# Turning x for the last stage by VectorE and DMAs instead of TensorE

## The chip, the cores and the metric

The kernel runs on one core of a Trainium2 chip. The metric is the device time of one execution in microseconds; several executions are timed and the median counts. The profile shows one execution, engine by engine: TensorE (PE, with its weight loads as PEld), VectorE (DVE), ScalarE (ACT), GpSimd (POOL) and SyncE (SP, which here only issues DMAs).

## The reference, cut to what matters

A decoder of two layers on 512 tokens of 1024 features. Each layer mixes (attention and retention) and then runs an MLP; a last RMS norm over the features of each token ends it. The change concerns the end of the second layer's MLP.

```python
D_MODEL = 1024; SEQ = 512; DEPTH = 2; D_FF = 4 * D_MODEL

def rmsnorm(x, g):
    xf = x.astype(jnp.float32)
    y = xf * lax.rsqrt(jnp.mean(xf * xf, axis=-1, keepdims=True) + EPS)
    return (y * g.astype(jnp.float32)).astype(x.dtype)

def hybrid_layer(x, g_mix, w_in, sinks, w_a, w_b, w_out, g_mlp, w_up, w_down):
    ...
    x = x + mixed @ w_out
    h2 = rmsnorm(x, g_mlp)
    x = x + jnp.square(jax.nn.relu(h2 @ w_up)) @ w_down
    return x

def reference(x, g_mix, w_in, sinks, w_a, w_b, w_out, g_mlp, w_up, w_down, g_final):
    for l in range(DEPTH):
        x = hybrid_layer(x, g_mix[l], w_in[l], sinks[l], w_a[l], w_b[l], w_out[l],
                         g_mlp[l], w_up[l], w_down[l])
    return rmsnorm(x, g_final)
```

## The kernel before, in words

All of x is kept turned: `x[:, c, :]` holds 128 features (chunk c of 8) in the partitions and the 512 tokens along the row. Weights come in units of 128x1024, 512 KB each, 46 units for `w_in` and so on in a fixed list (`unit_order`). SP loads a unit into a `raw` tile (three buffers), ACT copies it to `hi` (L286), a rounded form, DVE subtracts to get `lo` (L287), and every product is three matmuls, hi times hi, and hi times lo both ways (L332, L333, L334). Some projections are done in pairs of chunks with fewer products (`wide_pair`, L1336 and L1337): TensorE fills three PSUM banks a, b and e in turn, ACT copies b and e aside as `bu` and `eu` (L1370, L1366), copies a into b (L1363), and DVE joins them into `z` (L1343 to L1349, L1389), which is squared (L1409) and split into the two tiles of `up` (L339, L340).

The MLP of a layer goes by quarters of the 4096 hidden features. `mlp_sequence` puts them in order: for each quarter q below 3 and i from 0 to 3 first `two_chunks` for `w_down` of q, which adds two chunks of x (L1416), and then a pair of `w_up` for the next quarter. The three quarters finish all eight chunks of x but for the last quarter's share. In the second layer `end` does the last quarter with tokens in the partitions, so that the last norm can sum along rows and the output leaves by rows.

For that `end` needs x turned back. In the kernel before TensorE does it: `turned(f, b)` transposes four 128x128 pieces (L517) of half f (features 512f to 512f+511) and token block b into a PSUM bank. For f=0 ACT copies the four blocks out to `x0` (L527). Then the first half of the last stage multiplies four units of `w_down` (numbers 24 to 27, 96 matmuls) into four banks, and DVE adds them to `x0` (L550). For f=1 `seeded` copies the transposed block back into a `mm` bank (L543), on which the second half of the stage accumulates (`units` 28 to 31, split into `homes`, the tiles named r). ACT and DVE then square, scale and store. The pools: `tmp` with tag t has 6 buffers (side, eu, bu, gains, sq and others), `ps_mm` 5 banks and `ps_aux` 3.

The order on each engine is not the order of the code: a scheduler sorts all instructions by a time model of its own, and `tc.issue_after` holds one back until another has been issued. SP works strictly in its order, and a DMA that waits holds back those behind it.

Of the kernel before, what the change touches and what calls it, by code (L numbers as in the profile page):

```python
# [11 lines left out]
F32 = mybir.dt.float32  # L12
F32R = mybir.dt.float32r
AF = mybir.ActivationFunctionType
# [113 lines left out]
def decoder(ctx, tc, xT, x_first, w_in, w_a, w_b, w_out, w_up, w_down, tables, decay, band, triangles, g_last, out):  # L128
# [276 lines left out]

    def two_chunks(name, layer, moving, evacuates):

        banks = [bank(ps_mm, "mm") for _ in range(2)]
        for u in range(2):
            hi, lo = unit(name, layer)  # L410
            for j in range(4):
                k = 4 * u + j
                for c, ps in enumerate(banks):
                    cols = slice((2 * j + c) * P, (2 * j + c + 1) * P)
                    products(ps, [((hi[:, cols], lo[:, cols]), moving[k])], k == 0, k == KD - 1)
        for ps, evacuate in zip(banks, evacuates):
            evacuate(ps)
# [84 lines left out]


    def end(layer, uT):
        homes.extend(slots.four()[0] for _ in range(4))
# [6 lines left out]

        def turned(f, b, at=slice(0, T)):

            pt = bank(ps_aux, "xT")[:, : at.stop - at.start]
            for i, c in enumerate(range(at.start // P, at.stop // P)):
                nc.tensor.transpose(pt[:, i * P : (i + 1) * P], x[:, 4 * f + c, b * P : (b + 1) * P], ident)  # L517
            return pt

# [5 lines left out]

        for b in range(NB):
            nc.scalar.activation(x0[b], turned(0, b), AF.Copy)  # L527
        banks = [bank(ps_mm, "mm") for _ in range(NB)]
# [8 lines left out]

        H = T // 2
        steps = [(b, at) for b in range(NB) for at in ((slice(0, T),) if b < NB - 1 else (slice(0, H), slice(H, T)))]

        def seeded(b, at):
            ps = bank(ps_mm, "mm")[:, : at.stop - at.start]
            nc.scalar.activation(ps, turned(1, b, at), AF.Copy)  # L543
            return ps
# [3 lines left out]
        for b, ps in enumerate(banks):  # L548
            so_far = sums[b][:, 0:1]
            nc.vector.tensor_tensor(x0[b], x0[b], ps, ALU.add)  # L550
            nc.scalar.activation(temp("sq"), x0[b], AF.Square, accum_out=so_far)
            nc.vector.tensor_scalar(so_far, so_far, 1.0 / D, EPS, ALU.mult, ALU.add)
            nc.vector.tensor_tensor(x0[b], x0[b], gains[0], ALU.mult)
# [27 lines left out]
    def layer_body(layer):  # L581
# [842 lines left out]
        def first_hooks():  # L1424
# [4 lines left out]
            return {0: lambda: (rms_mlp.prepare(), sum_input(by_form, scaled_pair(0, g_mlp), 0)), 1: at1}  # L1429

        for what, q, i in mlp_sequence():
            if what == "first":
# [7 lines left out]
            elif what == "down":  # L1440
                two_chunks("w_down", layer, up[q], [put_down(2 * i), put_down(2 * i + 1)])
                if i == 3:
                    slots.give(*up_slots[q])
            elif layer == DEPTH - 1:
                end(layer, up[q])
            else:
                new_input()
                all_of(group("w_down", layer, up[q], [put_down(c, True) for c in range(4)]))
                for c in range(4, KD):
                    chunk("w_down", layer, up[q], put_down(c, True))  # L1450
                slots.give(*up_slots[q])
# [145 lines left out]
def _laid_out(x, g_mix, w_in, sinks, w_a, w_b, w_out, g_mlp, w_up, w_down, g_final):  # L1597
    r = np.arange
    wa_rows = np.concatenate([(4 * g + c) * HEAD_DIM + r(HEAD_DIM) for c in range(4) for g in range(2)])
    rotary, decay, band, triangles = _tables()  # L1600
# [38 lines left out]
```

## Time and profile before

| | us |
|---|---|
| median of 3 runs | 1473.04 |
| lowest and highest | 1472.45, 1473.24 |
| the profiled execution's own time | 1473.8 |
| its span, first to last instruction | 1472.0 |
| busy in it: PE, DVE, ACT | 1464.8, 1166.7, 810.9 |

The span is what the trace covers; the profiled execution's own time has 1.8 us more around it. A line of the timeline has the start in us from the span's start, the length, the engine, the line of the code, the operation, the tile written and the tiles read, the shape, and how often it stands there; in brackets how long the engine stood idle before it, and who ended that wait. Neighbouring matmuls overlap in the records, so TensorE's pace is read from one start to the next. The clock that TensorE was granted is 0.999 of full speed over the run.

### The profile page before, as it was taken

To read this page: it belongs to the slowest core of one execution; us is meant where nothing else is said; L and a number is where in the kernel's file an instruction comes from. 1 tells how busy PE (TensorE), PEld (TensorE's weight loads), DVE (VectorE), ACT (ScalarE), POOL (GpSimd) and SP (SyncE) were. 2 spreads that over 40 slices of the span, in tenths; PEclk is the share of its full clock that TensorE was granted. 3 is DMA by queue.
4 is the path that set the end of the run, shared out by engine and by line. 5 is a ranking of instruction groups with operands and counts; after the bars stand their busy time and mean duration, and the time that the engine had idled before them with its cause. 6 is when DMAs were issued, how large, how long until landed. Compare 5 with 4: busy or idle time off the path is not lost.

```text
span 1472.0 us, 20220 instructions
## 1 busy us (share of the span) xinstructions
PE 1464.8 (100%) x7466; PEld 1249.6 (85%) x7466; DVE 1166.7 (79%) x1920; ACT 810.9 (55%) x1306; POOL 3.8 (0%) x14
## 2 busy tenths in 40 slices
PE   9999999999999999999999999999999999999998
PEld 7888888888988888888888888888989888888887
DVE  7998878778988787776678986786899877878763
ACT  7656356654684445444455753656547754444553
POOL 0000000000000000000000000000000000000000
PEclk9999999999999999999999999999999999999999
DMA  6422843356443332333543258333654522333241
GB/s 227 127 89 92 300 158 99 102 172 212 126 126 118 101 115 93 104 104 115 165 126 97 86 186 272 104 104 102 207 171 126 154 95 93 114 106 109 90 140 57
DMA packets 71043, 194.45 MB, mean 132 GB/s; under 512 B 8457, under 2 KB 8609, under 8 KB 70945
## 3 DMA queue, kind: packets, MB, share of 16 engines
q1 hardware_dynamic: 70656, 192.65, 40.7%
q8 instruction: 58, 0.95, 0.3%
q10 hardware_dynamic: 288, 0.52, 0.1%
q14 instruction: 41, 0.33, 0.1%
HBM read 171.63 MB, written 18.89 MB: 129 GB/s over the span
## 4 chain that ended last, share of the span: by engine, by line
PE 94%; issue 5%; DMA 1%; DVE 0%; ACT 0%; POOLq 0%; DVEq 0%; SPq 0%
PE mm L334 22%; PE mm L332 22%; PE mm L333 22%; PE mm L1336 11%; PE mm L1337 5%; PE rv L332 2%; PE rv L333 2%; PE rv L334 2%; PE score L842 1%; PE r L332 1%; PE r L334 1%; PE r L333 1%; PE pT L797 0%; PE pv L823 0%; PE pv L824 0%
## 5 line engine op out<-in xcount | busy, mean ns | idle before, releaser
L333 PE MATMUL mm<-r,hi 128*128 128x512 f32 (+1 forms) x1568 | 572.5, 367 | 0.0
L332 PE MATMUL mm<-r,hi 128*128 128x512 f32 (+1 forms) x1568 | 569.7, 367 | 0.6 <-ACT r L342 0.6
L334 PE MATMUL mm<-r,lo 128*128 128x512 f32 (+1 forms) x1568 | 563.9, 367 | 0.2
L286 ACT ACTIVATE hi<-raw 128x1024 fp32r<-128x1024 f32 (+1 forms) x334 | 334.1, 1002 | 386.4 <-PE mm L333 206.8
L287 DVE TENSOR_TENSOR lo<-raw,hi 128x512 fp32r<-128x512 f32 (+1 forms) x335 | 384.7, 1151 | 111.6 <-ACT hi L286 107.9
L334 PEld LDWEIGHTS mm<-r,lo 128*128 128x128 f32 x1568 | 293.7, 188 | 48.7 <-DVE lo L287 1.4
L332 PEld LDWEIGHTS mm<-r,hi 128*128 128x128 f32 x1568 | 293.8, 188 | 47.5 <-ACT r L342 1.4
L333 PEld LDWEIGHTS mm<-r,hi 128*128 128x128 f32 x1568 | 294.3, 188 | 45.9
L1336 PE MATMUL mm<-r,hi 128*128 128x512 f32 x728 | 252.1, 391 | 0.0
L1337 PE MATMUL mm<-r,lo 128*128 128x256 f32 x728 | 200.5, 277 | 0.0
L1336 PEld LDWEIGHTS mm<-r,hi 128*128 128x128 f32 x728 | 136.5, 188 | 28.6
L1337 PEld LDWEIGHTS mm<-r,lo 128*128 128x128 f32 x728 | 136.7, 188 | 3.1 <-DVE lo L287 0.7
L1416 DVE TENSOR_TENSOR x<-x,mm 128x512 f32<-128x512 f32 x56 | 37.8, 686 | 28.9 <-PE mm L334 28.9
L1409 ACT ACTIVATE z<-z 128x512 f32<-128x512 f32 x56 | 32.4, 623 | 48.7 <-DVE z L1389 48.7
L333 PE MATMUL rv<-lo,r 128*128 128x512 f32 x128 | 49.8, 389 | 0.0
L334 PE MATMUL rv<-hi,r 128*128 128x512 f32 x128 | 49.5, 389 | 0.0
L332 PE MATMUL rv<-hi,r 128*128 128x512 f32 x128 | 49.4, 390 | 0.0
L340 DVE TENSOR_TENSOR r<-z,r 128x512 fp32r<-128x512 f32 x64 | 42.9, 686 | 3.0 <-ACT r L339 2.6
L339 ACT ACTIVATE r<-z 128x512 fp32r<-128x512 f32 x64 | 38.4, 619 | 7.9 <-DVE z L1070 7.8
L869 ACT ACTIVATE sm<-sm,st 128x256 f32<-128x256 f32 (+1 forms) x64 | 30.1, 472 | 18.9 <-DVE st L857 18.7
L1389 DVE SCALAR_TENSOR_TENSOR z<-z,rstd 128x512 f32<-128x512 f32 x52 | 35.7, 687 | 0.6
L340 DVE TENSOR_TENSOR r<-sums,r 128x1024 fp32r<-128x1024 f32 x24 | 28.9, 1220 | 0.0
(273 smaller groups left out, 1693.0 us busy)
## 6 DMA issues: line engine op xcount, KB each, us to landing
raw<-w_in_in SPq DMA_DIRECT2D x89, 512.0 KB, 3.7
raw<-w_down_in SPq DMA_DIRECT2D x64, 512.0 KB, 3.6
raw<-w_up_in SPq DMA_DIRECT2D x32, 512.0 KB, 4.0
raw<-w_up_in SPq DMA_DIRECT2D x60, 256.0 KB, 2.9
raw<-w_a_in SPq DMA_DIRECT2D x8, 512.0 KB, 4.8
ahead<-w_b_in SPq DMA_DIRECT2D x8, 512.0 KB, 5.4
park_w_b<-ahead SPq DMA_DIRECT2D x16, 256.0 KB, 5.7
ahead<-w_up_in SPq DMA_DIRECT2D x8, 512.0 KB, 4.9
```

The costliest lines, as they stand in the source:

```text
L286: nc.scalar.activation(hi[:, at], raw[:, at], AF.Copy)
L287: last_low[:] = [nc.vector.tensor_tensor(lo[:, at], raw[:, at], f32(hi[:, at]), ALU.subtract).ins]
L332: nc.tensor.matmul(ps, ah, bh, start=start and i == 0, stop=False, **more)
L333: nc.tensor.matmul(ps, ah, bl, start=False, stop=False, **more)
L334: nc.tensor.matmul(ps, al, bh, start=False, stop=stop and i == n - 1, **more)
L339: nc.scalar.activation(hi, src, AF.Copy)
L340: nc.vector.tensor_tensor(lo, src, f32(hi), ALU.subtract)
L1336: nc.tensor.matmul(both, hi[:, c], m, start=start and k == 0, stop=False, **more)
L1337: nc.tensor.matmul(ps[:, :H], lo[:, c], m[:, 0, :], start=False, stop=k == 3 and start, **more)
L1389: nc.vector.scalar_tensor_tensor(z[:, :, at], z[:, :, at], 0.0, factor, ALU.max, ALU.mult)
L1409: nc.scalar.activation(z[:, i, :], z[:, i, :], AF.Square)
L1416: nc.vector.tensor_tensor(x[:, c, :], x[:, c, :], ps, ALU.add)
```

## The change

The 32 transposes on TensorE, ACT's copies out of PSUM for f=0 and the function `turned` go. Instead `turns(f)` makes four steps. Step n takes all four chunks of half f, picks 32 tokens of each of the four token blocks, and turns them on DVE in blocks of 32x32 into a temporary tile `turned` of 128x512 (line 516 of the new code); SP writes it to a part of the HBM tensor `blocks` (line 517), 256 KB. At the fourth step SP issues four DMAs that read `blocks` back into x itself, each into 32 partitions with 4 rows of 512 values (line 520). After that x holds the half with tokens in the partitions. The 32x32 blocks leave the features in another order, so the host permutes features in `x`, `w_out`, `g_mix`, `w_in`, `g_mlp`, `w_up` and most of `w_down` such that the output comes out in its own order.

For f=0 the four steps stand behind the units of `two_chunks` for (q, i) = (2, 2) and (2, 3); for f=1 they stand at the head of `end`. DVE's addition for f=0 (line 569) and ACT's seeding for f=1 (line 562) now read x in SBUF.

```diff
-    def two_chunks(name, layer, moving, evacuates):
+    def two_chunks(name, layer, moving, evacuates, meanwhile=None):
...
+            if meanwhile:
+                with tc.issue_after(last_low[0]):
+                    meanwhile.pop(0)()
...
+    blocks = dram.tile([2, P, 4, T], F32, name="blocks")
+
+    def turns(f):
+
+        four = x[:, 4 * f : 4 * f + 4, :]
+
+        def turn(n):
+            new = temp("turned")
+            old = four.rearrange("p c (b r j) -> p c b r j", b=NB, j=32)[:, :, :, n, :]
+            nc.vector.transpose(new.rearrange("p (b c j) -> p c b j", b=NB, j=32), old)
+            nc.sync.dma_start(blocks[f, :, n, :], new)
+            if n == 3:
+                for r in range(4):
+                    nc.sync.dma_start(four[32 * r : 32 * r + 32], blocks[f, :, r, :].rearrange("(a p) w -> p a w", a=4))
+
+        return [partial(turn, n) for n in range(4)]
...
-        def turned(f, b, at=slice(0, T)):
-
-            pt = bank(ps_aux, "xT")[:, : at.stop - at.start]
-            for i, c in enumerate(range(at.start // P, at.stop // P)):
-                nc.tensor.transpose(pt[:, i * P : (i + 1) * P], x[:, 4 * f + c, b * P : (b + 1) * P], ident)
-            return pt
+        def by_rows(ap):
+            return ap.rearrange("p (a w) -> p a w", w=P)
+
+        def by_tokens(f, b):
+            return x[:, 4 * f : 4 * f + 4, b * P : (b + 1) * P]
+
+        with tc.issue_after(last_low[0]):
+            all_of(turns(1))
...
-        for b in range(NB):
-            nc.scalar.activation(x0[b], turned(0, b), AF.Copy)
...
-            nc.scalar.activation(ps, turned(1, b, at), AF.Copy)
+            nc.scalar.activation(by_rows(ps), by_tokens(1, b)[:, at.start // P : at.stop // P, :], AF.Copy)
...
-            nc.vector.tensor_tensor(x0[b], x0[b], ps, ALU.add)
+            nc.vector.tensor_tensor(by_rows(x0[b]), by_tokens(0, b), by_rows(ps), ALU.add)
...
+                if (layer, q, i) == (DEPTH - 1, 2, 2):
+                    turning = turns(0)
+                two_chunks("w_down", layer, up[q], [put_down(2 * i), put_down(2 * i + 1)], turning)
...
+    turned = r(D).reshape(2, 4, 4, 32).transpose(0, 2, 1, 3).reshape(-1)
+    x, w_out = (m[:, :, turned] for m in (x, w_out))
+    g_mix, w_in, g_mlp, w_up = (m[:, turned] for m in (g_mix, w_in, g_mlp, w_up))
```

The scheduler's order is the same up to the last 100 us or so, but for numbers in names. Lines from L403 on have moved in the new code: L1336 and L1337 of before are L1355 and L1356 there, L1363 is L1382, L1366 is L1385, L1370 is L1389 on ACT, L1389 on DVE is L1408, L1343 is L1362.

First place: the last pair (q = 3, i = 3), TensorE and ACT. TensorE before, with the banks b = mm_12719, a = mm_12720, e = mm_12721; L517 are the transposes:

```order
L1336 MATMUL mm_12720<-r12_88,hi_12660 128x512
L1337 MATMUL mm_12720<-r12_88,lo_12661 128x256
L517 MATMUL xT_12841<-ident_132,x_75 128x128 x4
L517 MATMUL xT_12847<-ident_132,x_75 128x128 x4
L517 MATMUL xT_12853<-ident_132,x_75 128x128 x4
L1336 MATMUL mm_12721<-r8_84,hi_12660 128x512
```

The same place of the change, where e is mm_12738:

```order
L1356 MATMUL mm_12737<-r12_88,lo_12668 128x256
L1355 MATMUL mm_12737<-r12_88,hi_12667 128x512
L1356 MATMUL mm_12737<-r12_88,lo_12668 128x256
L1355 MATMUL mm_12738<-r8_84,hi_12667 128x512
L1356 MATMUL mm_12738<-r8_84,lo_12668 128x256
```

Nothing stands any more between the products of bank a and those of bank e. ACT at this place before, from the copy of a into b on:

```order
L1363 ACTIVATE mm_12719<-mm_12720 128x512
L286 ACTIVATE hi_12730<-raw3_12727 128x1024
L286 ACTIVATE hi_12754<-raw_12602 128x512
L1366 ACTIVATE eu_12722<-mm_12721 128x512
L1370 ACTIVATE bu_12723<-mm_12719 128x512
L286 ACTIVATE hi_12780<-raw_12725 128x1024
```

and now:

```order
L1382 ACTIVATE mm_12736<-mm_12737 128x512
L1385 ACTIVATE eu_12739<-mm_12738 128x512
L286 ACTIVATE hi_12747<-raw3_12744 128x1024
L286 ACTIVATE hi_12771<-raw_12609 128x512
L1389 ACTIVATE bu_12740<-mm_12736 128x512
L286 ACTIVATE hi_12797<-raw_12742 128x1024
```

The copy `eu` has moved ahead of the two splits of the pair's last weights (raw3 and its neighbour).

Second place: SP from the loads of the last pair (L223 to L225) to the end of the loads. Before:

```order
L223 DMA raw<-w_up_in 128x512
L228 DMA raw_12630<-w_up_in 128x512
L225 DMA raw<-w_up_in 128x1024
L196 DMA raw<-w_down_in 128x1024 x5
L508 DMA gains<-g_last_in 128x512 x2
L196 DMA raw<-w_down_in 128x1024 x3
```

and now:

```order
L517 DMA blocks<-turned 128x512 x2
L223 DMA raw<-w_up_in 128x512
L228 DMA raw_12637<-w_up_in 128x512
L225 DMA raw<-w_up_in 128x1024
L196 DMA raw<-w_down_in 128x1024
L517 DMA blocks<-turned 128x512 x2
L520 DMA x<-blocks 32x4x512 x4
L196 DMA raw<-w_down_in 128x1024 x4
L528 DMA gains<-g_last_in 128x512 x2
L517 DMA blocks<-turned 128x512 x3
L196 DMA raw<-w_down_in 128x1024 x3
L517 DMA blocks<-turned 128x512
L520 DMA x<-blocks 32x4x512 x4
```

The four writes and four reads for f=0 stand among the loads of the last pair and of unit 25; for f=1 three writes stand ahead of the last three loads (units 29 to 31), the fourth and the four reads behind them.

Third place: DVE in the last pair, from the first norm scaling of its z on. Before:

```order
L1389 SCALAR_TENSOR_TENSOR z<-z,rstd 128x2x256
L287 TENSOR_TENSOR r_76<-raw,r_76 128x1024
L287 TENSOR_TENSOR lo<-raw,hi 128x1024
L1343 TENSOR_TENSOR z<-mm,side 128x256
L287 TENSOR_TENSOR lo<-raw,hi 128x1024
L1389 SCALAR_TENSOR_TENSOR z<-z,rstd 128x2x256
```

and now:

```order
L1408 SCALAR_TENSOR_TENSOR z<-z,rstd 128x2x256
L516 STREAM_TRANSPOSE turned<-x 128x4x4x32 x3
L287 TENSOR_TENSOR r_76<-raw,r_76 128x1024
L287 TENSOR_TENSOR lo<-raw,hi 128x1024
L1362 TENSOR_TENSOR z<-mm,side 128x256
L287 TENSOR_TENSOR lo<-raw,hi 128x1024
L516 STREAM_TRANSPOSE turned<-x 128x4x4x32
L1408 SCALAR_TENSOR_TENSOR z<-z,rstd 128x2x256
```

Three turns stand ahead of the split of unit 28 (r_76), the fourth behind that of unit 27. For f=0 the four turns stand in the same manner behind two splits each in the two pairs of steps before.

More of the change, by code (lines that the diff above doesn't have):

```diff
@@ L535, in end @@
                     multiply(ps, k, b, weights, k == 0, k == KD - 1)
-        H = T // 2
         steps = [(b, at) for b in range(NB) for at in ((slice(0, T),) if b < NB - 1 else (slice(0, H), slice(H, T)))]
@@ L1429, in first_hooks @@
             return {0: lambda: (rms_mlp.prepare(), sum_input(by_form, scaled_pair(0, g_mlp), 0)), 1: at1}
+        turning = []
         for what, q, i in mlp_sequence():
@@ L1440, in layer_body @@
             elif what == "down":
-                two_chunks("w_down", layer, up[q], [put_down(2 * i), put_down(2 * i + 1)])
+                if (layer, q, i) == (DEPTH - 1, 2, 2):
+                    turning = turns(0)
+                two_chunks("w_down", layer, up[q], [put_down(2 * i), put_down(2 * i + 1)], turning)
                 if i == 3:
@@ L1598, in _laid_out @@
     r = np.arange
+    turned = r(D).reshape(2, 4, 4, 32).transpose(0, 2, 1, 3).reshape(-1)
+    x, w_out = (m[:, :, turned] for m in (x, w_out))
+    g_mix, w_in, g_mlp, w_up = (m[:, turned] for m in (g_mix, w_in, g_mlp, w_up))
+    w_down = w_down.copy()
+    w_down[:, : 3 * D] = w_down[:, : 3 * D, turned]
+    w_down[: DEPTH - 1, 3 * D :] = w_down[: DEPTH - 1, 3 * D :, turned]
     wa_rows = np.concatenate([(4 * g + c) * HEAD_DIM + r(HEAD_DIM) for c in range(4) for g in range(2)])
```

## The prediction

> **What bounds the kernel now.** I read the page's busy time first, then the chain that ended last, then the waits of TensorE.
>
> ```profile
> span 1472.0 us, 20220 instructions
> PE 1464.8 (100%) x7466; PEld 1249.6 (85%) x7466; DVE 1166.7 (79%) x1920; ACT 810.9 (55%) x1306; POOL 3.8 (0%) x14
> PE 94%; issue 5%; DMA 1%; DVE 0%; ACT 0%; POOLq 0%; DVEq 0%; SPq 0%
> PE warm L311 <- DVE ones L306: 1.0, 1, 1.0
> PE mm L332 <- ACT r L342: 0.6, 1, 0.6
> ```
>
> TensorE is busy for the whole span, the chain lies on it for 94%, and it waits twice in 1472.0 us, for 1.0 and 0.6 us. So work taken off TensorE shortens the run by its own time, unless what feeds the matmuls behind it was only just ready. Both halves of that are worked out below: first what leaves TensorE, then whether DVE, ACT or the transfers are late for a TensorE that runs ahead.
>
> **What leaves TensorE.** The transposes are one group, and the timeline of TensorE shows the largest and one of the single ones among their neighbours (start, duration).
>
> ```profile
> L517 PE MATMUL xT<-ident,x x32: 270/272/273, 1410.7 to 1460.6; 128*128 128x128 f32 x32
> 1410.33 0.39 PE L1336 MATMUL mm<-r,hi 128*128 128x512 f32 x1
> 1410.55 0.28 PE L1337 MATMUL mm<-r,lo 128*128 128x256 f32 x1
> 1410.67 1.47 PE L517 MATMUL xT<-ident,x 128*128 128x128 f32 x12
> 1411.90 0.47 PE L1336 MATMUL mm<-r,hi 128*128 128x512 f32 x1
> 1412.21 0.28 PE L1337 MATMUL mm<-r,lo 128*128 128x256 f32 x1
> 1443.09 0.40 PE L334 MATMUL mm<-hi,r 128*128 128x512 f32 x1
> 1443.32 0.27 PE L517 MATMUL xT<-ident,x 128*128 128x128 f32 x1
> 1443.35 0.48 PE L332 MATMUL mm<-r,r 128*128 128x512 f32 x1
> 1443.66 0.40 PE L333 MATMUL mm<-r,r 128*128 128x512 f32 x1
> ```
>
> Each has 0.27 us, but matmuls overlap, so the duration isn't what one costs. From the first L1336 to its L1337 go 0.22 us (1410.33 to 1410.55). From the twelve transposes to the second L1337 behind them go 1.54 us (1410.67 to 1412.21), of which one L1336 takes 0.22: the twelve cost 1.32, 0.11 each. The single one: 1443.32 to 1443.66 is 0.34 with one L332, and the L334 ahead of it, a matmul of the same form, takes 0.23 (1443.09 to 1443.32), so 0.11 again. 32 x 0.11 = **3.5 us** off TensorE. 24 of the 32 stand before 1443.35, so TensorE comes 24 x 0.11 = 2.6 us earlier to the second half of the last stage, and 12 x 0.11 = 1.3 us earlier to what stands behind the first group.
>
> **What DVE takes on.** Eight STREAM_TRANSPOSE of 128x512 float32. The trace holds none; the nearest rows are DVE's other operations, below with their idle time in brackets.
>
> ```profile
> 1403.57 1.23 DVE L287 TENSOR_TENSOR lo<-raw,hi 128x1024 fp32r<-128x1024 f32 x1 [1.90 <-ACT hi L286]
> 1405.46 1.23 DVE L287 TENSOR_TENSOR lo<-raw,hi 128x1024 fp32r<-128x1024 f32 x1 [0.67 <-ACT hi L286]
> 1408.81 1.37 DVE L1416 TENSOR_TENSOR x<-x,mm 128x512 f32<-128x512 f32 x2 [1.07 <-PE mm L334]
> 1426.60 1.23 DVE L287 TENSOR_TENSOR r<-raw,r 128x1024 fp32r<-128x1024 f32 x1 [4.71 <-ACT r L286]
> 1432.48 1.23 DVE L287 TENSOR_TENSOR r<-raw,r 128x1024 fp32r<-128x1024 f32 x1 [1.45 <-ACT r L286]
> 1450.76 0.49 DVE L571 TENSOR_SCALAR o<-o,st 128x512 f32<-128x512 f32 x1
> ```
>
> 128x512 takes 0.49 with one input and 0.69 with two (half of L1416's 1.37); 128x1024 takes 1.23. My bounds for a turn are 0.49 and 1.23 us (as though each value went through twice), and I take 0.69, the usual price of that many float32. Eight make 5.5 us, at the upper bound 9.8. DVE isn't the bound, so only the places count. The f=1 turns one to three go into the 4.71 us ahead of 1426.60 (2.1 us, at most 3.7: hidden), the fourth stands ahead of the 1.45 us before 1432.48 (hidden either way). Of the f=0 turns the last two stand behind the split of 1403.57; the idle 0.67 and 1.07 us after it take up 1.4 at 0.69, but at 1.23 leave 0.7 us late, and that runs into the place below. If the idle time weren't there, DVE's split chain would be late by the whole turn.
>
> The Trainium skill, page "VectorE: DVE Perf Modes", section "The three transpose paths", gives 311 ns for a 128x128 turn in 32x32 blocks on VectorE and 390 ns on TensorE, and its rules for authors prefer TensorE for 128x128 into PSUM. By its figure a turn here would be, as an estimate, 4 x 311 = 1.24 us; the 0.11 us per transpose above is well under its TensorE figure, and no run here shows its VectorE one.
>
> **The tight place.** Behind the twelve transposes the last pair's second weights, raw3, still have to be split into hi (ACT) and lo (DVE).
>
> ```profile
> 1412.02 1.06 ACT L286 ACTIVATE hi<-raw 128x1024 fp32r<-128x1024 f32 x1 [0.57 <-DVE raw L260]
> 1413.99 0.58 ACT L1366 ACTIVATE eu<-mm 128x512 f32<-128x512 f32 x1
> 1414.99 0.60 ACT L1370 ACTIVATE bu<-mm 128x512 f32<-128x512 f32 x1 [0.42 <-PE mm L1337]
> 1413.12 1.83 DVE L287 TENSOR_TENSOR lo<-raw,hi 128x1024 fp32r<-128x1024 f32 x2 [0.53 <-ACT hi L286]
> 1416.09 0.39 PE L1336 MATMUL mm<-r,hi 128*128 128x512 f32 x1
> ```
>
> TensorE begins on these weights at 1416.09, with 1.3 us less at 1414.8, and at the lo part 0.2 later. The order now puts the copy eu ahead of hi. Its bank is complete four pairs behind 1411.90, at some 0.34 a pair (1410.33 to 1410.67) near 1413.3, now 1412.0. So eu runs to 1412.6, hi 1.06 more to 1413.7, lo 1.23 more to 1414.9; bu has to wait for a second hi of 0.6 and ends 0.6 later, 1414.9 to 1415.1. Both land within 0.2 us of when TensorE wants them (lo, and the bank that bu empties). I take 0.2 us lost, between nothing and 0.4; with turns at 1.23 the additional 0.7 makes it 0.9.
>
> **The transfers for f=0.** Four writes and four reads of 256 KB are added to SP's queue between 1402 and 1411 and wait for turns, so the loads behind them on SP could be late. The load nearest behind them that counts is that of unit 28.
>
> ```profile
> 1421.31 0.33 SPq L196 DMA_DIRECT2D raw<-w_down_in  x1
> 1425.51 1.06 ACT L286 ACTIVATE r<-raw 128x1024 fp32r<-128x1024 f32 x1 [5.01 <-DMA raw<-w_down_in]
> 1402.00:1411.00 9.00, 9.00 (x47) 7.63 (x46) 5.66 (x8) 4.72 (x8) 0.00 (x0) 1.00 0.03 13
> 1431.00:1434.00 3.00, 3.00 (x15) 2.49 (x14) 1.26 (x2) 2.61 (x4) 0.00 (x0) 1.00 0.86 333
> 1434.50:1439.00 4.50, 4.50 (x22) 3.69 (x22) 3.57 (x4) 2.03 (x4) 0.00 (x0) 1.00 0.00 0
> 1434.44 1.14 ACT L339 ACTIVATE r<-z 128x512 fp32r<-128x512 f32 x2
> 1437.76 0.48 PE L332 MATMUL mm<-hi,r 128*128 128x512 f32 x1
> ```
>
> In the windows (the last two columns are the DMA engines' share and GB/s) the engines stand at 0.03 in 1402 to 1411, so 2 MB in and out have room, 15 us before x is used. Load 28 is issued at 1421.31 because its buffer comes free then; it stays ahead of the f=1 writes in the order, so ACT's 5.01 us wait ends as before. Cost nothing; if SP were held up by a turn past 1421, load 28 and all behind it would move by that. Unit 27's input r is written by 1435.0 (1434.44 plus 0.57, half of 1.14) for TensorE at 1437.76, now 1435.2; its chain starts from a TensorE bank that also comes earlier (1.3 us by then), so r ends near 1434.0 and 1.2 us are left.
>
> **The transfers for f=1.** Here the new path ends in the seed of PSUM, ACT's L562, which no longer reads TensorE's xT but x as the four reads bring it back. The nearest rows (KB each, median to landing):
>
> ```profile
> spill<-x SPq DMA_DIRECT2D x8, 256.0 KB, 2.1
> x<-spill SPq DMA_DIRECT2D x8, 256.0 KB, 3.8
> park_w_up<-ahead SPq DMA_DIRECT2D x16, 256.0 KB, 7.3
> x<-xT_in SPq DMA_DIRECT2D x15, 256.0 KB, 5.9
> r<-qlo SPq DMA_DIRECT2D x32, 64.0 KB, 2.8
> 1430.35 0.69 DVE L1389 SCALAR_TENSOR_TENSOR z<-z,rstd 128x512 f32<-128x512 f32 x1
> ```
>
> The fourth turn stands where the scaling of 1430.35 stands, so it ends near 1430.35 + 0.69 - 1.3 = 1429.8, say 1430.0. Its write queues behind the last loads, which keep the engines at 0.86 and 333 GB/s until 1434; I let it land at 1434.4, since the 2.1 us of a write are over by then. The reads issue at 1434.5 into empty engines (0.00 until 1439): 3.8 us gives 1438.3, the seed (0.58, as L1366) 1438.9. TensorE wants it at 1443.35 - 2.6 = 1440.7: 1.8 us of slack, cost nothing. From the other side, a write of 7.3 and a read of 5.9, from the issue at 1430.2, give 1430.2 + 13.2 + 0.6 = 1444.0 and a stall of 3.3. I take the quick pair, because the slow rows come from stretches full of loads, and these engines are empty.
>
> **What leaves ACT.** Four copies of 0.60 (L527), and the adds and seeds read SBUF in place of PSUM.
>
> ```profile
> L527 ACT ACTIVATE x<-xT x4: 592/598/608, 1417.4 to 1419.9; 128x512 f32<-128x512 f32 x4
> ```
>
> These 2.4 us lie behind the tight place and nothing waits for them: gain nothing. The permuted features cost nothing on the chip: the same instructions, tiles and sizes.
>
> **The sum.** 3.5 off, 0.2 back: 3.3 us. The profiled execution has a span of 1472.0 and a time of its own of 1473.8, 1.8 over the span and 0.8 over the median 1473.04. The span goes to 1468.7, the execution to 1470.5, and the median of the runs to **1469.7**.
>
> **Rivals.**
> 1. *The tight place costs more.* Turns at 1.23 us: 0.9 lost in place of 0.2, so 1470.4. For it: a block turn may not move as fast as an addition. Against: the idle time above, and that nothing later needs the lost 0.7.
> 2. *The read-back into 32 partitions goes at half rate.* 1 MB at half of the 333 GB/s takes 6.3 us: 1434.5 + 6.3 + 0.6 = 1441.4, a stall of 0.7, 1470.4. With the slow write and read above a stall of 3.3 gives 1473.0, no change. For it: each read reaches a quarter of the partitions. Against: two different reads may run side by side. The Trainium skill, page "SBUF — State Buffer", section "Door 1: The DMA port swizzle", says that a transfer into 32 partitions reaches only 8 of 16 ports; that rule is this half rate, and no row here shows its effect by itself.
> 3. *Slower: the seed waits for the read-back.* The mechanism is one place, L562, behind fourth turn, write and four reads. If 256 KB in 32 partitions cost what r<-qlo's 64 KB in 32 partitions do per byte, 4 x 2.8 = 11.2 us, and the four go two at a time, the reads take 22.4: 1434.5 + 22.4 + 0.6 = 1457.5, a stall of 16.8, 1486. It turns to slower once the seed ends after 1440.7 + 3.5 + 2.9 = 1447.1. For it: it is the only chain here with four dependent steps. Against: 2.8 us for a small transfer is mostly its latency, which four together share.
> 4. *The change does not do what it says:* the work that leaves TensorE was hidden in overlap, so that less than 3.5 comes off. Against: 0.11 is the distance between neighbours, not a duration. It would give about 1472.
>
> **How the numbers follow.** Forecast .56, with a range of its own of 1469.3 to 1470.1 (0 to 0.6 lost, 0.2 of spread). Rival 1 .15, rival 2 .11, rival 3 .16, rival 4 .02. About 0.2% (2.9 us) is what a measurement can tell here: faster is below 1470.1, same up to 1476. Rival 1 falls on either side of that line, mostly into same; faster is the forecast and .02 of it, .58; same is the rest of rivals 1, 2 and 4, .26; slower is .16. The range for 8 in 10: from 1468.9 (no loss, and 0.02 us more per transpose) to 1474.5, which holds rivals 1, 2 and 4 and the mild end of rival 3.
>
> **What would show it.** TensorE's xT rows gone and its busy time down by some 3.5 us; STREAM_TRANSPOSE rows near 0.69 (forecast) or 1.23 (rival 1); TensorE's waits with at most 0.3 us for L1355 and its neighbours behind raw3; the reads of blocks landing by 1438.5 and the first L562 before TensorE's banks of unit 28. A wait of TensorE on L562 of over 1 us means rival 2, of several us rival 3. The forecast is wrong if turns take longer than 1.23 us or the f=1 write lands after 1437.

## The result and the profile after

The change takes 1470.95 us (median of 22 runs, 1469.73 to 1471.64), the kernel before 1473.11 beside it (22 runs, 1472.29 to 1473.73). The ratio is 0.9986, with a 95% interval of 0.9979 to 0.9992: 2.2 us faster, between 1.2 and 3.1. That is clear of no change, less than the 3.3 us of the forecast, and less than the 0.2% that the prediction called faster. The time lies in the range given (1468.9 to 1474.5), but 0.85 us above the likeliest case's own 1469.3 to 1470.1. The nearest times given were the 1470.4 of rivals 1 and 2.

The page of the profiled execution, with the same three lines that the prediction shows of before:

```profile
span 1469.4 us, 20189 instructions
PE 1461.8 (99%) x7434; PEld 1246.4 (85%) x7434; DVE 1171.2 (80%) x1928; ACT 809.4 (55%) x1302; POOL 3.8 (0%) x14
PE 94%; issue 5%; DVE 1%; DMA 0%; ACT 0%; POOLq 0%; DVEq 0%; SPq 0%
```

TensorE has 3.0 us less work and is still the engine the end hangs on. But it now waits in a place where it did not before. The waits of TensorE's matmuls over the whole run, then those of its weight loads (PEld) from 1380 us on; in the profile of before the second list is empty:

```profile
PE warm L311 <- DVE ones L306: 1.0, 1, 1.0
PE mm L332 <- ACT mm L562: 0.9, 1, 0.9
...
PEld mm L332 <- ACT mm L562: 1.3, 1, 1.3
PEld mm L332 <- ACT r L339: 0.6, 1, 0.6
PEld mm L1355 <- ACT mm L1382: 0.2, 1, 0.2
```

The list of weight loads tells more than that of matmuls: a wait that a matmul in the pipeline partly covers is left out of the first list (L339) or shortened in it (L562). Three places give time back: L1382, the copy of a bank in the pair ahead of the last one; L339, the input of unit 27; and L562, the seed that reads x as it comes back from HBM.

How much each gives back is read by matching the matmuls of the two traces one by one, without the transposes (7434 on either side), and subtracting the start times. This table is worked out from the traces, not a view of the page:

```
start before   before - after   what lies between
       6.30        0.82         (start of the run)
    1394.83        0.62         behind L1382
    1412.55        1.88         12 transposes gone: +1.26
    1425.69        2.73         8 more gone: +0.85
    1443.34        1.68         4 more gone, less the waits for L339 and L562
    1460.66        2.53         8 more gone: +0.85
```

The first row is not the change's: the two executions differ by 0.8 us before 7 us are over (the wait of 0.6 for ACT's r L342 in the profile of before is absent here). Between 0.82 and the last row lie 1.7 us, where 32 transposes at 0.106 are 3.4. Lost are 0.2 at L1382 and 3.2 - 1.68 = 1.5 at L339 and L562 together (without them the offset at 1443.34 would be 0.62 + 24 x 0.106 = 3.2). The start of the run varies like that between executions, so offsets say what a change does in one execution, and the medians what it is worth.

The loss at L1382 starts on DVE. These are the second turn of a pair, the scaling of z behind it and ACT's copy in the change, then the same scaling and copy before:

```profile
1385.26 0.71 DVE L516 STREAM_TRANSPOSE turned<-x 128x512 f32<-128x512 f32 x1
1386.31 0.69 DVE L1408 SCALAR_TENSOR_TENSOR z<-z,rstd 128x512 f32<-128x512 f32 x1
1390.09 0.58 ACT L1382 ACTIVATE mm<-mm 128x512 f32<-128x512 f32 x1
...
1386.57 0.69 DVE L1389 SCALAR_TENSOR_TENSOR z<-z,rstd 128x512 f32<-128x512 f32 x1
1390.39 0.58 ACT L1363 ACTIVATE mm<-mm 128x512 f32<-128x512 f32 x1
```

TensorE of the change is 0.86 us ahead of before at 1380, but the scaling is only 0.26 ahead and the copy 0.30.

The turns, and ACT from load 30's split to the first seed (in brackets the idle time ahead and what ended it):

```profile
L516 DVE STREAM_TRANSPOSE turned<-x x8: 667/702/706, 1383.4 to 1429.5; 128x512 f32<-128x512 f32 x8
...
1433.41 1.06 ACT L286 ACTIVATE r<-raw 128x1024 fp32r<-128x1024 f32 x1 [0.89 <-DMA raw<-w_down_in]
1434.38 1.13 ACT L339 ACTIVATE r<-z 128x512 fp32r<-128x512 f32 x2
1435.80 1.06 ACT L286 ACTIVATE r<-raw 128x1024 fp32r<-128x1024 f32 x1 [0.28 <-DMA raw<-w_down_in]
...
1441.00 0.60 ACT L562 ACTIVATE mm<-x 128x512 f32<-128x512 f32 x1 [4.14 <-DMA x<-blocks]
```

A turn takes 0.70 us. ACT idles 0.89 us for load 30, whose split stands ahead of L339, and so r comes late for TensorE; and ACT sits idle for 4.14 us until x is back. TensorE around the two waits:

```profile
1434.52 0.39 PE L334 MATMUL mm<-hi,ulo 128*128 128x512 f32 x1
1435.05 0.50 PE L332 MATMUL mm<-hi,r 128*128 128x512 f32 x1
...
1441.66 0.50 PE L332 MATMUL mm<-r,r 128*128 128x512 f32 x1 [0.88 <-ACT mm L562]
```

SP's queue shows the order of the transfers at the end:

```profile
1426.98 2.93 SPq L196 DMA_DIRECT2D raw<-w_down_in  x3
1430.20 0.33 SPq L517 DMA_DIRECT2D blocks<-turned  x1
1430.62 6.13 SPq L520 DMA_DIRECT2D x<-blocks  x4
```

The reads do not wait for the whole half: read r takes what write r put down, so three of them are issued at 1430.6 to 1431.9, right behind the fourth write, and the fourth one at 1436.45, when that write has landed. The questions for the experiments: is it the late fourth write that makes the seed late, or reads into 32 partitions that are slow, and are the three losses the turning's at all?

### The profile page after: what moved, and what is told of

Same layout as the page of the kernel before. It is cut to its first block, busy times and chain, and to the rows that moved or that the text cites. A ratio compares the mean times of both kernels' runs of the same rounds, so it can differ in the third digit from the quotient of the medians.

```text
span 1469.4 us, 20189 instructions
## 1 busy us (share of the span) xinstructions
PE 1461.8 (99%) x7434; PEld 1246.4 (85%) x7434; DVE 1171.2 (80%) x1928; ACT 809.4 (55%) x1302; POOL 3.8 (0%) x14
## 4 chain that ended last, share of the span: by engine, by line
PE 94%; issue 5%; DVE 1%; DMA 0%; ACT 0%; POOLq 0%; DVEq 0%; SPq 0%
PE mm L334 22%; PE mm L332 22%; PE mm L333 22%; PE mm L1355 10%; PE mm L1356 5%; PE rv L332 2%; PE rv L334 2%; PE rv L333 2%; PE score L861 1%; PE r L332 1%; PE r L334 1%; PE r L333 1%; PE pT L816 0%; PE pv L843 0%; PE pv L842 0%
## 5 line engine op out<-in xcount | busy, mean ns | idle before, releaser
L1355 PE MATMUL mm<-r,hi 128*128 128x512 f32 x728 | 252.1, 391 | 0.0
L1356 PE MATMUL mm<-r,lo 128*128 128x256 f32 x728 | 200.4, 277 | 0.0
L1355 PEld LDWEIGHTS mm<-r,hi 128*128 128x128 f32 x728 | 136.5, 188 | 28.8 <-ACT mm L1382 0.2
L1356 PEld LDWEIGHTS mm<-r,lo 128*128 128x128 f32 x728 | 136.7, 188 | 3.2 <-DVE lo L287 0.6
L339 ACT ACTIVATE r<-z 128x512 fp32r<-128x512 f32 x64 | 38.2, 618 | 8.0 <-DVE z L1089 8.0
L1408 DVE SCALAR_TENSOR_TENSOR z<-z,rstd 128x512 f32<-128x512 f32 x52 | 35.6, 685 | 0.6
```

The costliest lines, as they stand in the source:

```text
L339: nc.scalar.activation(hi, src, AF.Copy)
L1355: nc.tensor.matmul(both, hi[:, c], m, start=start and k == 0, stop=False, **more)
L1356: nc.tensor.matmul(ps[:, :H], lo[:, c], m[:, 0, :], start=False, stop=k == 3 and start, **more)
L1408: nc.vector.scalar_tensor_tensor(z[:, :, at], z[:, :, at], 0.0, factor, ALU.max, ALU.mult)
```

## The experiments

The runs came in three groups, each beside runs of the kernel before on the same chip (medians 1472.97, 1473.29 and 1472.72).

| kernel | us (median) | ratio to before, 95% |
|---|---|---|
| the change | 1470.95 | 0.9986 (0.9979 to 0.9992) |
| none | 1468.93 | 0.9973 (0.9962 to 0.9983) |
| writes | 1469.08 | 0.9975 (0.9965 to 0.9985) |
| wide | 1469.96 | 0.9981 (0.9973 to 0.9990) |
| early4 | 1469.40 | 0.9976 (0.9966 to 0.9985) |
| f0 | 1471.13 | 0.9985 (0.9977 to 0.9994) |
| f1 | 1472.18 | 0.9992 (0.9983 to 1.0002) |
| chunks | 1488.34 | 1.0100 (1.0087 to 1.0114) |
| chunks_early4 | 1483.90 | 1.0070 (1.0057 to 1.0083) |
| swap | 1470.86 | 0.9987 (0.9978 to 0.9996) |
| late4 | 1470.88 | 0.9987 (0.9978 to 0.9996) |
| dve2 | 1472.15 | 0.9996 (0.9987 to 1.0005) |
| best | 1471.78 | 0.9996 (0.9987 to 1.0005) |

The outputs of none, writes and wide are not the reference's: they leave out part of the turning, or put x back in another place.

Beside the medians, the matching of TensorE's starts gives what each profiled execution gains on before from 1380 us, where the kernels begin to differ, to 1460. This is worked out from the traces: none 3.7, writes 3.5, early4 3.5, wide 2.5, the change 1.7, f0 1.7, late4 1.5, swap 1.4, best 1.0, f1 0.9, dve2 0.8.

### No turning at all (none)

```diff
-                if (layer, q, i) == (DEPTH - 1, 2, 2):
-                    turning = turns(0)
...
-        with tc.issue_after(last_low[0]):
-            all_of(turns(1))
```

> Leaves out: the turning of x for both halves (no DVE turn, no write, no read-back; the last stage reads x untransposed, so the output is not the reference's). TensorE's order is that of the change. Theory A (32 transposes of 0.105 to 0.11 us are worth 3.4 us and the turning path gives back 1.3 of it): TensorE's waits for L562 (0.9) and ACT's r L339 (0.6 in the weight loads) and the 0.2 behind ACT's L1382 are all gone, 1473.1 - 3.4 = 1469.7, 1.2 below the change. Rival B (TensorE in front just runs into the next thing, its own weight loads and ACT's splits, whatever turns x): the wait for r L339 stays, 0.3 to 0.6, and the time is 1470.1 to 1470.5.

Measured: 1468.93, 4.0 us below its before (2.5 to 5.6). Of the three waits none is left; TensorE's weight loads wait for nothing from 1380 on. Matched with before, the offset goes from 0.67 at 1380 us to 4.36 at 1460, so by 3.7, where 32 x 0.11 are 3.5. So what leaves TensorE is worth its 3.5 us in full, and the change gives back about 2 us, by the medians (1470.95 - 1468.93) as by the matching (3.7 - 1.7). Theory A had only 1.3 given back, and 1469.7. On rival B this run says less than it was meant to: without the read-back the seed is ready early, and the order took the products of units 28 and 29 ahead of those of unit 27, so that r L339 is wanted later here. That expectation's remark on TensorE's order was wrong.

### Turns and writes without the read-back (writes)

```diff
-            if n == 3:
-                for r in range(4):
-                    nc.sync.dma_start(four[32 * r : 32 * r + 32], blocks[f, :, r, :].rearrange("(a p) w -> p a w", a=4))
```

> Leaves out: the eight read-backs (DVE turns and writes stay; the last stage reads x untransposed, so the output is not the reference's). Theory A1 (what gives time back is the read-back: its reads gate the seed and crowd the loads): no wait for L562, time as without any turning, 1469.7 to 1470.0. Rival A2 (the f=1 writes ahead of the last loads make loads 28 and 30 late): ACT's r L339 is still waited for with 0.6, load 30 lands 5 us or more after its issue, 1470.1 to 1470.3.

Measured: 1469.08, as good as none; the one wait left is the 0.2 behind ACT's copy (L1379 here). DVE's eight turns and 2 MB of writes cost 0.2 us, the reading back costs the rest. A1 holds; A2's wait for r L339 is absent, but this order too had moved units 28 and 29 forward, so A2 is not refuted by it.

### The same bytes into 128 partitions (wide)

```diff
-                    nc.sync.dma_start(four[32 * r : 32 * r + 32], blocks[f, :, r, :].rearrange("(a p) w -> p a w", a=4))
+                    nc.sync.dma_start(four[:, r, :], blocks[f, :, r, :])
```

> Changes what is computed: the four reads put block row r into all 128 partitions of one chunk in place of 32 partitions of four chunks, same bytes and same packets of 2 KB, so the output is not the reference's. Theory H (reads into 32 partitions run at a lower rate: 186 GB/s at a DMA share of 0.87 where loads get 333 at 0.86): the rate behind 1435 rises to near 330 GB/s, the reads land by 1439.5, no or nearly no wait for L562, 1470.0. Rival L (the fourth write lands late, at 1436.4, behind load 31 and beside the first three reads, and the fourth read can only start then): the wait for L562 stays at 0.5 or more, 1470.5 to 1471.

All engines' order is that of the change. The windows around the f=1 reads, of the change first (last two columns: share of the DMA engines' time, GB/s):

```profile
1435.00:1436.00 1.00, 0.95 (x4) 0.82 (x5) 1.00 (x2) 0.72 (x2) 0.00 (x0) 1.00 1.05 256
1436.00:1437.00 1.00, 1.00 (x7) 0.80 (x6) 1.00 (x3) 0.86 (x1) 0.00 (x0) 1.00 0.98 213
```

and of this kernel:

```profile
1435.00:1436.00 1.00, 0.81 (x4) 0.68 (x5) 1.00 (x2) 1.00 (x3) 0.00 (x0) 1.00 1.02 393
```

With the engines full, 32 partitions take 256 and 213 GB/s, 128 take 393. The packets show it too, worked out from the traces: the median packet of 2 KB takes 153 ns in these two windows of the change, and 84 ns in that of wide. The wait for L562 is gone and 1.0 us of the time with it (1469.96); the reads landed by 1439.08. What TensorE waits for now is the other place:

```profile
PEld mm L332 <- ACT r L339: 1.0, 1, 1.0
PEld mm L1355 <- ACT mm L1382: 0.2, 1, 0.2
```

H held, and for the rate it named. This agrees with the rule weighed in the prediction (the Trainium skill, "SBUF — State Buffer", "Door 1: The DMA port swizzle"): 32 partitions reach half of the ports. Its half is the harder figure; measured here are 0.54 to 0.65 of the rate (213 and 256 of 393).

### The fourth turn with its own buffer (early4)

```diff
-            new = temp("turned")
+            new = big("turned")[:, 0, :] if f == 1 and n == 3 else temp("turned")
```

> The fourth turn of f=1 gets a buffer of its own, so that it no longer waits for the first write; the order then puts all four turns, the four writes and two reads ahead of load 29, the other two behind it. Rival L (late fourth write): the read-back is over by 1433, the wait for L562 is gone, +1.0 us of the gain comes back, 1470.0; if the reads make loads 29 to 31 late, TensorE waits for ACT's r L339 or for the r splits instead. Theory H (32 partitions at a low rate): the reads still take 4 to 5 us in all, but in a place where they gate loads 30 and 31, whose splits then come late: a wait of 1 us or more for DVE's or ACT's r, 1470.5 to 1471.5.

Measured: 1469.40. All ten runs (1468.73 to 1469.71) lie below the lowest of the change's 22: this is the fastest kernel that computes the whole reference, faster than before by 3.6 us (2.2 to 5.0). SP's queue shows why:

```profile
1424.62 2.43 SPq L520 DMA_DIRECT2D x<-blocks  x2
1427.10 0.42 SPq L196 DMA_DIRECT2D raw<-w_down_in  x1
1427.62 0.86 SPq L520 DMA_DIRECT2D x<-blocks  x2
1428.52 1.20 SPq L196 DMA_DIRECT2D raw<-w_down_in  x2
```

All reads stand ahead of loads 30 and 31 now. These land 4 and 3 us later than in the change (1437.4 and 1438.7), but ACT's first seed runs at 1436.46, and the order has put one r L339 and this seed between the splits, which wait for the loads without anyone waiting for them:

```profile
1434.93 0.61 ACT L339 ACTIVATE r<-z 128x512 fp32r<-128x512 f32 x1
1436.46 0.60 ACT L562 ACTIVATE mm<-x 128x512 f32<-128x512 f32 x1 [0.92 <-issue]
1437.46 1.06 ACT L286 ACTIVATE r<-raw 128x1024 fp32r<-128x1024 f32 x1 [0.40 <-DMA raw<-w_down_in]
1438.70 1.06 ACT L286 ACTIVATE r<-raw 128x1024 fp32r<-128x1024 f32 x1 [0.17 <-DMA raw<-w_down_in]
```

Of TensorE's waits only the 0.2 behind L1382 is left. No wait for L562 is what theory L forecast, with 1470.0; the time is 0.6 us better than that. Whether for its reason is taken up with late4.

### One half each (f0, f1)

f0 keeps TensorE's transposes in the seeds, f1 those for x0; the host permutes only the features of the half that DVE turns.

```diff
-        with tc.issue_after(last_low[0]):
-            all_of(turns(1))
...
-            nc.scalar.activation(by_rows(ps), by_tokens(1, b)[:, at.start // P : at.stop // P, :], AF.Copy)
+            nc.scalar.activation(ps, turned(1, b, at), AF.Copy)
```

> Half of the change: f=0 is turned by DVE and HBM, f=1 stays with TensorE (16 transposes in the seeds). Theory L (what gives back is the f=1 read-back and the loads beside it): 16 x 0.11 = 1.76 off, 0.1 to 0.2 back behind ACT's copy L1382, none at L562 or r L339, 1473.0 - 1.6 = 1471.4. Rival (f=0's reads into 32 partitions, 228 GB/s at full share in front of loads 26 to 28, make these late): TensorE waits for a split of unit 26 to 28 or for r L339, 0.3 or more, 1471.7 to 1472.

Measured: 1471.13, 2.2 us below its before (0.9 to 3.4); the only wait is the 0.2 behind ACT's copy. Half of the change gains as much as all of it. The rival, loads 26 to 28 made late by f=0's reads, shows nowhere.

> The other half: f=1 is turned by DVE and HBM, f=0 stays with TensorE (16 transposes). 1.76 off in all, but only 8 x 0.11 = 0.9 of it stand ahead of the second half of the last stage, so TensorE wants the seed 1.7 us later than in the change. Theory L (the seed waits only because TensorE got ahead of a read-back that ends at a fixed time): no wait or at most 0.2 for L562, 1471.3 to 1471.5. Rival (the read-back is late by its own order, behind loads and writes that move with TensorE): the wait for L562 stays at 0.5 or more, 1472 or more. The order has the three first writes behind load 30 here and not ahead of load 29, which speaks a little for the rival.

Measured: 1472.18, not clear of before. Theory L, which here says that the read-back ends at a fixed time, fell, and the rival was right: TensorE waits 0.5 for the seed (1.0 in the weight loads) and its weight loads 0.3 for r L339, though it wanted the seed 1.7 us later. The order had put the three first writes behind load 30, the reads are issued at 1433.65 and later, and the last one lands at 1441.4 (1440.9 in the change). The end of the read-back goes by where the order puts it.

### Reading by chunks (chunks, chunks_early4)

The same result by way of all 128 partitions: each read fetches one chunk from all four written blocks. chunks_early4 adds the buffer of early4.

```diff
-                for r in range(4):
-                    nc.sync.dma_start(four[32 * r : 32 * r + 32], blocks[f, :, r, :].rearrange("(a p) w -> p a w", a=4))
+                for a in range(4):
+                    nc.sync.dma_start(four[:, a, :], blocks[f, 32 * a : 32 * a + 32].rearrange("p r w -> r p w"))
```

> Each read-back takes one chunk in all 128 partitions, from all four written blocks, in place of 32 partitions of four chunks from one block: same result, same bytes, same 2 KB packets. All four f=1 reads now have to wait for the fourth write. Theory H and L together: the rate at full share is 385 GB/s as in the kernel with wide reads and not 245; the fourth write lands at 1435 (no reads beside it), the reads by 1439.6, the first seed by 1440.2, the wait for L562 is 0 to 0.3 in place of 0.9, 1470.2. If the late write alone were the cause (L without H) the four reads would take the 4.5 us and more that one took and L562 waits 1 us or more, 1471 or more.

> Chunk-wise reads, and the fourth f=1 turn with its own buffer: all four writes go ahead of load 29, the reads stand between loads 30 and 31. Theory L: no wait for L562, the seed is ready by 1437; the wait for ACT's r L339 (load 30's split stands ahead of it on ACT, and load 30 lands beside the writes) stays at 0.3 to 0.6; 1469.5 to 1469.8. If the reads delay load 31, its split r_81 comes late for TensorE near 1447, over 0.5 us: 1470 or more; in the kernel with an early fourth write its split ended at 1439.8, so I don't expect it.

Measured: 1488.34 and 1483.90, 15 and 10 us slower than before; both expectations missed by far, and both theories had nothing to say on it. The window in chunks in which f=0's reads run alone:

```profile
1411.50:1416.00 4.50, 4.50 (x28) 3.95 (x27) 3.71 (x7) 3.67 (x6) 0.00 (x0) 1.00 0.27 91
```

A share of 0.27 is 4.3 of 16 engines, and each of these reads has four completions of its data in the trace, where the others have 16: each is spread over four engines, and the loads queue behind it on these four (of the first load's 16 completions twelve are in by 1419.3, the last four come at 1425.6 to 1426.4). The source of these reads has an outermost dimension of 4, both sides of the reads in the change and in wide 32 or 128. The Trainium skill says so ("DMA: Bandwidth & Descriptors", section "Rules for kernel authors", row "Use all 16 engines"): an outermost dimension below 16 confines a DMA to at most that many engines. The trace agrees. TensorE then waited 6.8 us for the seed in chunks, 2.7 for a split and 2.6 for r L339. This is the slower rival of the prediction, a seed gated by its read-back, brought about by another cause.

### ACT's split of load 30 behind L339 (swap)

```diff
+                    if i == len(order) - 2:
+                        with tc.issue_after(last_hi[0]):
+                            nc.scalar.activation(hi[:, at], raw[:, at], AF.Copy)
+                    else:
-                    nc.scalar.activation(hi[:, at], raw[:, at], AF.Copy)
+                        nc.scalar.activation(hi[:, at], raw[:, at], AF.Copy)
...
-            nc.scalar.activation(hi, src, AF.Copy)
+            last_hi[:] = [nc.scalar.activation(hi, src, AF.Copy).ins]
```

> ACT's split of load 30 goes behind the two r L339 copies; nothing else on ACT, SP and in the transfers moves. Theory G (the read-back ends at a fixed time, about 1441, and the seed's wait takes up whatever TensorE wins ahead of it): the wait for r L339 is gone, the wait for L562 grows from 0.9 to about 1.3, the time stays at 1470.9. Rival (the two waits cost time each for itself): L562 stays at 0.9, 1470.5.

Measured: 1470.86, no different from the change. The waits of TensorE, and of its weight loads (the lines have moved by 6):

```profile
PE mm L338 <- ACT mm L568: 1.7, 1, 1.7
...
PEld mm L338 <- ACT mm L568: 2.1, 1, 2.1
PEld mm L1361 <- ACT mm L1388: 0.2, 1, 0.2
```

The wait for r is gone and the seed's has grown by 0.8, more than the 0.4 expected; with SP's order as in the change the last read landed at 1440.5, against 1440.9. The time is what theory G forecast: the wait for r costs nothing by itself as long as the seed behind it is later still. The two are not to be added; only in a kernel without the seed's wait (wide) does the first one count.

### The fourth write twice (late4)

```diff
+            if f == 1 and n == 3:
+                nc.sync.dma_start(spare, new)
             nc.sync.dma_start(blocks[f, :, n, :], new)
```

> The fourth f=1 turn is written twice, first to a spare tensor of 256 KB, then to blocks; no engine's order moves but SP's by this one write. Theory L (the late fourth write gates the last read-back and with it TensorE): 256 KB at 350 GB/s are 0.75 us, and so much is added to the wait for L562, 0.9 to 1.6, 1471.6. Rival (some slack or another wait decides): under 0.3 more, 1471.2 or less.

Measured: 1470.88; the wait for the seed (L565) is 0.7, not 1.6, and that for r L339 0.5 (0.9 in the weight loads, 0.6 in the change). Theory L's forecast missed. The table, worked out from the traces, has when the transfers were over: the last of the 16 completions of each.

```
                     load 31   4th write   read 0    read 1    read 2    read 3 (issued)
the change           1435.78   1436.44     1437.63   1438.86   1439.85   1440.90 (1436.45)
late4                1434.23   1435.65     1436.89   1438.05   1439.20   1440.28 (1435.66)
wide                 1435.03   1435.72     1436.38   1437.02   1437.63   1439.08 (1435.74)
```

In the change the four reads end 1.0 to 1.2 us apart, and the fourth one in the same step as the others, though it was issued 4 us later: when it is issued, none of reads 0 to 2 is over yet. 256 KB in 1.1 us are 240 GB/s. In wide the step is 0.6, and only there does the fourth read stand out, by 1.45. So in the change the fourth read loses little by being late, but not nothing. Between its issue and its end the DMA engines had room, as windows of the change show (last two columns: their share, GB/s):

```profile
1437.00:1438.00 1.00, 1.00 (x6) 0.84 (x5) 1.00 (x1) 0.00 (x0) 0.00 (x0) 1.00 0.87 186
1438.00:1439.00 1.00, 1.00 (x6) 0.84 (x5) 0.12 (x1) 0.00 (x0) 0.00 (x0) 1.00 0.74 186
1439.00:1440.00 1.00, 1.00 (x6) 0.81 (x5) 0.00 (x0) 0.00 (x0) 0.00 (x0) 1.00 0.25 59
```

From 1436 to 1439 about 0.4 us of their time went unused (0.02 + 0.13 + 0.26); as an estimate, that is what an earlier fourth read could have gained, less than half of the seed's 0.9.

Late4 itself does not settle it. Load 31 landed 5.0 us after its issue and not 6.2, so the fourth write came earlier than in the change and not later; and a queue ahead of the reads would have grown by the doubled write as well. Why load 31 was quicker, and why the median of 11 runs did not move either, stays open. What is shown is that the seed waits for four slow reads queued behind the last loads: the wait goes when the reads are faster (wide), and when that queue stands ahead of loads that can wait (early4). That early4 wins by this rather than by sparing the fourth read its wait is argued from the steps above; no run moves the fourth write alone.

### Every turn twice (dve2)

```diff
             nc.vector.transpose(new.rearrange("p (b c j) -> p c b j", b=NB, j=32), old)
+            nc.vector.transpose(new.rearrange("p (b c j) -> p c b j", b=NB, j=32), old)
```

> Each DVE turn is done twice into the same tile: 8 x 0.70 = 5.6 us more DVE work. If the turns are hidden as predicted, but for the second of each f=0 pair, which pushes DVE's scaling and with it ACT's copy L1382: the wait for L1382 grows from 0.2 to 0.9, the tight place at raw3 loses up to 0.7, the f=1 turns cost nothing by themselves; 1471.5 to 1472.5. If turns cost their own time (rival): 1476.

Measured: 1472.15, 1.2 above the change for 5.6 us of DVE work, inside the span expected, but not for the reasons given. L1382's wait is gone; 0.4 is lost behind the copy bu of the tight place; and the doubled f=1 turns do cost: they push two writes behind load 29 and one behind load 30, so the reads are issued at 1434.8 to 1437.3, and the seed's wait in the weight loads goes from 1.3 to 1.6, that for r from 0.6 to 1.1.

### Early fourth turn, and f=0's second turn behind the scaling (best)

On top of early4's edit:

```diff
-                with tc.issue_after(last_low[0]):
+                with tc.issue_after(last_z[0] if u else last_low[0]):
                     meanwhile.pop(0)()
...
-                nc.vector.scalar_tensor_tensor(z[:, :, at], z[:, :, at], 0.0, factor, ALU.max, ALU.mult)
+                last_z[:] = [nc.vector.scalar_tensor_tensor(z[:, :, at], z[:, :, at], 0.0, factor, ALU.max, ALU.mult).ins]
```

> The kernel with the early fourth f=1 turn, and the second f=0 turn of each pair of steps behind DVE's scaling of z, whose order then moves a little around it on TensorE and ACT too. Expected: the 0.2 behind ACT's copy L1382 is gone as well, no wait of TensorE but the first; 1469.2, against 1469.4 with the early turn alone and 1468.9 without any turning. If the later second turn makes the split of raw3 late: 0.3 or more for DVE's lo L287, 1469.7.

Measured: 1471.78, a miss. The 0.2 behind the copy is gone as expected, but the order at the end moved as well: the three other f=1 writes went behind load 29 (1427.5) and the last two reads behind load 31, and TensorE waits 2.1 us for the seed. Its weight loads also wait 0.4 for DVE's lo, but at 1429.8, well behind raw3. A gain of 0.2 in one place cost 2 in another, through the order alone.

## Why the prediction was right, and where it was not

- **What leaves TensorE, 3.5 us**: right. By the matching 3.7 were gained in none and 3.5 in writes, and 0.106 each where they were counted in the change. This also answers rival 4: the work was not hidden.
- **What DVE takes on, 0.69 a turn, hidden but for the last f=0 turns**: right in size (0.70), and writes shows that turns and writes together cost 0.2. The estimate of 1.24 by the Trainium skill ("VectorE: DVE Perf Modes", "The three transpose paths", a figure for bf16) is not borne out: 512 columns of float32 took 0.70. Nor is its preference for TensorE ("Rules for kernel authors"), where TensorE bounds the kernel and DVE has time to spare: with the early fourth turn the way by DVE and HBM is 3.6 us faster than TensorE's transposes (early4).
- **The tight place at raw3, 0.2 lost**: right in size by luck, wrong in place. Nothing waits there; the 0.2 is lost in the pair ahead of it, where f=0's second turn delays DVE's scaling and so ACT's copy L1382. The prediction counted 1.07 us of idle time to take up that turn, but this idle time stands behind the scaling.
- **The transfers for f=0, nothing**: right (f0).
- **r L339, slack 1.2**: wrong. I moved its chain forward with TensorE, but on ACT it stands behind the split of load 30, and the loads do not come earlier with TensorE: load 30 landed at 1433.4 (before: 1433.5), and TensorE was held up 0.3 to 0.4 us. In the sum it costs nothing, since the seed's wait takes it up (swap).
- **The transfers for f=1, slack 1.8**: the step that failed. It had the write landing at 1434.4 and then reads of 3.8 us into empty engines, over by 1438.3. The engines were not empty: three reads, which need only writes 0 to 2, went in behind load 31, the last write landed at 1436.44, 2.0 us later than that, and the four reads at some 240 GB/s were over only 4.5 us after it, at 1440.90. The seed ended at 1441.6, 2.7 us later than forecast, where 1.8 were there to spare. The rates came from rows of transfers with 128 partitions.
- **Rival 2**, slow reads into 32 partitions, at .11 with 1470.4, had the right place and half of the mechanism. Its seed ended at 1441.4, close to the 1441.6, but partly by luck: the reads were faster than its half rate (4.5 us and not 6.3 behind the write) and the write was 2.0 us later. The seed cost TensorE 0.9 by its list of waits, against the 0.7 of this rival; with r's wait it was 1.5.
- **The time**: the range held because it had room for rivals 1 and 2. The forecast of 3.3 us came out as 2.2 because of the f=1 transfers.
- **The slower rival**: it did not come about here, but its mechanism is real: in chunks, with a read-back some four times slower than the engines allow, the seed waits 6.8 us.

## What to carry to other kernels

When work leaves the bounding engine, list what feeds the matmuls behind it and ask of each whether it comes earlier too: here loads and read-backs did not, and half of the change (f0) was worth as much as all of it. Price a transfer by rows with the same number of partitions and the same outermost dimension, and count what queues on the DMA engines ahead of it; a transfer in a full queue was moved forward here by ordering it ahead of what can wait (early4). Look at the order again after each edit, since one that frees 0.2 us in one place can move transfers in another for 2 (best).

## What the runs showed of the hardware

- DVE turns 128x512 float32 in blocks of 32x32 in 0.70 us, as long as an addition of that size (0.69).
- With full DMA engines, reads from HBM into 32 partitions ran at 213 to 256 GB/s, the same bytes and packets into 128 at 393 (median 2 KB packet 153 against 84 ns). The reads to partitions 0 to 31 and 32 to 63 came one after the other here; whether another order of the four makes them faster was not tried.
- Reads with a source whose outermost dimension is 4 ran at 91 GB/s, at an engine share of 0.27, on four engines.
